# Moving the side work of a hybrid encoder layer to other steps of its weight stream

## The chip, the cores and the metric

The program runs on one core of one Trainium2 chip. The metric is the device time of one execution in microseconds (us), lower is better; of several runs the median counts. The kernel before took 1551.28 us (median of 3 runs, 1549.84 to 1552.31).

## The reference: what is computed

One encoder layer on 256 tokens of width 4096, all in float32.

```python
h = layer_norm(x, emb_g, emb_b)
p = h @ w_in                       # 4096 -> 13312: c_b, c_c, c_h, c_z (2048 each), q (2048), k, v (512 each), a_z (2048)
y_conv = c_b * centred_short_conv(c_c * c_h, conv_w) * silu(c_z)
y_attn = banded_window_attention(q, k, v, sink) * silu(a_z)   # 16 heads of 128, 4 kv heads, window 128, ALiBi
y = concat([y_conv, y_attn]) @ w_out                           # 4096 -> 4096
out = layer_norm(2 ** 0.25 * h + y, ln_g, ln_b)
```

Nearly all arithmetic is in the two projections, `w_in` and `w_out`; their weights are read from memory once. The 256 rows give only two 128-row tiles, so each weight that arrives is used at once and dropped.

## The kernel before, in words

**A stream of weights.** The program is a list of steps (`IN_STEPS`, 304 of them, and 72 `OUT_STEPS`). The output columns are cut into chunks of 512 (26 chunks for `w_in`, in the order K, V, then AZ and Q for each of four groups of heads, then CC, CH, CZ, CB for each of four groups of convolution channels; `w_out` follows). A chunk's contraction of 32 k-tiles is cut into steps of three kinds:

- a *piece* (`s`): four k-tiles, 1 MB of weights, 24 matmuls with 512 columns (`mm`, L241 to L243);
- a *pair* (`S`): two k-tiles multiplied by Strassen's scheme, 0.5 MB, 21 matmuls with 256 columns (`mm_pair`, L265 to L267) where the plain way would need 24 of these;
- a *half* (`h`): two k-tiles the plain way, 12 matmuls with 512 columns.

A chunk of seven pairs runs as `sSShSsSSsSSs` (12 steps). K and V have eight pieces and no pair. A pair needs sums of blocks of the activations, made once for each pair number by `x_sums` (L628), and sums of blocks of the weights, made for each pair by `sums` (L180 to L182).

**Splitting.** Every weight w is split into w_hi and w_lo (`split_hi` on ScalarE, L199; `split_lo` on VectorE, L203), and each product is made of three matmuls: hi with hi, hi with lo, lo with hi. `whi` and `wlo` have three buffers each. So `split_hi(j + 3)` can start when step j's matmuls are done, `split_lo(j + 3)` follows it, and step j + 3 needs both: its first matmul the hi part, its second the lo part.

**What sets the order.** All four engines run their instructions strictly in the order in which the program is written. At step j the loop writes: the matmuls of j (TensorE), `split_hi(j + 3)` (ScalarE), then whatever was entered for step j in a table with `at(step, function)`, then the weight loads (SyncE's queue), then `sums(j + 4)` and `split_lo(j + 3)` (VectorE). The table `later` holds all *side work*: attention, convolution, and the ends of chunks. Work entered at step j therefore stands on TensorE behind the matmuls of j, on ScalarE behind `split_hi(j + 3)`, and on VectorE ahead of `split_lo(j + 3)`.

**The side work.** At a chunk's end `pair_copy` and `pair_sums` (L661, L668 to L671) put the Strassen products together and `whole` (L676, two instructions) adds the plain ones; `whole` belongs to `chunk_end`, written at the first step of the next chunk. Call that step base + 0. From there:

- a CH or CB chunk gets `product` (L681), four transposes on TensorE for each of two halves (L480), and `conv_mul` or `gate_mul` on VectorE;
- a CZ or AZ chunk gets a SiLU on ScalarE (`s_act` L710, `z_act` L523, the latter with a table load), an AZ chunk also transposes (`z_tr`);
- a Q chunk gets a group of four heads, numbered 0 to 3 here. `SPREAD` lists, for each head, the offsets of nine stages: scores (TensorE, L550 to L552), `s_add` (VectorE, L557, L559, L561), `exps` (ScalarE, L570, L571), `recip` (VectorE, L576, L578), `norms` (ScalarE, L584), `p_tr` (four transposes on TensorE, L591, and a copy to `pT` on ScalarE, L593), `p_lo` (VectorE, L598), `pv` (six matmuls, L605 to L607) and `out_z` (VectorE, L611, and a store). The queries are turned and split by `q_tr` and `q_lo` (L540), once for each two heads. A group spreads over two chunks: offsets 0 to 11 lie in the next AZ chunk (or CC), 12 to 23 in the next Q chunk (or CH).

**Buffers that the side work shares.** In the pool `pa` every tile has one buffer, unless it says otherwise: `s` (scores with bias), `pT` (transposed probabilities) and `zT` have one each, `p` has two. PSUM has two buffers named `att`, in turn for the transposed queries, scores, transposed probabilities and `pv`'s result; four `acc` and two `pacc` for the projections.

```python
    ps_att = pps.enter_context(tc.tile_pool(name="ps_att2", bufs=2, space=PSUM))
    pa = ph.enter_context(tc.tile_pool(name="pa", bufs=1))
        t = pa.tile([P, 2, 2, S], F32R, name="pT")
        nc.scalar.activation(t[:, 0, :, :], t_ps, AF.Copy)
```

**The end.** The last two output chunks have 256 columns. `res_load` brings the residual's rows; for the last chunk it issues seven loads on SyncE's queue, ahead of the last weight load.

Of the kernel before, what the change touches and what calls it, by code (L numbers as in the profile page):

```python
# [14 lines left out]
P = 128  # L15
# [25 lines left out]
HW = W // 2  # L41
HT = S // 2
NP = 7
PAIRS = [0, 0] + [NP] * (len(IN_ORDER) - 2)
ORDERS = {0: "s" * 8, NP: "sSShSsSSsSSs"}
OUT = 100
OP = 4
OUT_ORDERS = ["s" * 8] * 2 + ["sSsSsSsSss"] * 4 + ["s" * 8, "", ""]
# [49 lines left out]
def encoder_kernel(ctx: ExitStack, tc: tile.TileContext, x, emb_g, emb_b, wi, ws, conv_w, sink, wo, ln_g, ln_b, out):  # L98
# [516 lines left out]
    def head(n, *steps):  # L615
        return [(t, f, n) for t, f in zip(steps, (scores, s_add, exps, recip, norms, p_tr, p_lo, pv, out_z))]

    SPREAD = [(2, q_tr, 0), (3, q_lo, 0), (7, q_tr, 1), (8, q_lo, 1)] + head(0, 4, 5, 6, 7, 8, 9, 10, 12, 13) + head(
        1, 6, 7, 8, 9, 10, 12, 13, 15, 16) + head(2, 10, 11, 12, 13, 14, 17, 18, 20, 21) + head(
        3, 14, 15, 16, 17, 18, 19, 20, 22, 23)  # L620

    def open_pc():
        nonlocal pc
# [114 lines left out]
    def y_lo(q):  # L738
        for hi, lo, y in y_parts(q):
            nc.vector.tensor_tensor(lo, y, hi.bitcast(F32), op=ALU.subtract)  # L740

    build_tab()
    later = {}

# [6 lines left out]
    def chunk_end(j, ci):  # L751
        c0, fn = next((c, f) for c, f in ENDS if IN_ORDER[ci] >= c)
        g = IN_ORDER[ci] - c0
        fn(ci, g)
        if fn is end_k:
            at(j + 1, k_turn, g)
        if fn is end_cz:
            at(j + 1, s_act)
        if fn is end_z:
            at(j + 1, z_act)  # L760
            for b in range(2):
                at(j + 16 + b, z_tr, b) if g else at(j + 5 + b, z_tr, b)
        if fn is end_q:
            h = g * GROUP
            for t, f, a in SPREAD:
                at(j + t, f, a if f in (q_tr, q_lo) else h + a)
            if g < 2:
                at(j + 15, k_load, g)
                at(j + 23, v_load, g)
        if fn in (end_ch, end_cb):  # L770
            key, other, tr, mul = ("u", "c", conv_tr, conv_mul) if fn is end_ch else ("g", "s", gate_tr, gate_mul)
            last = ci == len(IN_ORDER) - 1
            if last:
                product(key, other)
            else:
                at(j + 2, product, key, other)
            for t, f, b in ((2, tr, 0), (2, tr, 1), (3, mul, 0), (3, mul, 1)) if last else (
                    (4, tr, 0), (5, tr, 1), (5, mul, 0), (7, mul, 1)):
                at(j + t, f, g, b)

    c_ch0 = IN_ORDER.index(C_CH)
# [8 lines left out]
    for j in range(n_pro, N_IN):  # L790
        kind, ci, q = steps[j]
        if j == z0 - 18:
            extra.clear()
        if j == z0 + 6:
            extra.insert(0, (pw, "w6"))
        mm_pair(j) if kind == "pair" else mm(j)
        split_hi(j + 3)
        for fn, a in later.pop(j, []):
            fn(*a)
        if kind == "pair" and q == PAIRS[ci] - 1:  # L800
            pair_copy(ci)
            at(j + 1, pair_sums, ci)
        if ci == 1 and q >= 2 or ci == 2 and j < NPC + 2 + NP:
            x_sums(j - NPC - 2, pa.tile([P, 4 * S], F32, name="xs", tag="zT"))
        if steps[j + 1][1] != ci or j == N_IN - 1:
            if ci == c_ch0:
                at(j + 4, open_pc)
            if PAIRS[ci]:
                at(j + 1, chunk_end, j + 1, ci)
            else:  # L810
                chunk_end(j, ci)
        loads(j)
        sums(j + 4)
        split_lo(j + 3)
# [180 lines left out]
    for n, (c0, w, pk, j0) in enumerate(chunks):  # L995
        us = out_units(n)
        np_ = sum(u[0] == "opair" for u in us)
        for t, (kind, _, q) in enumerate(us):
            j = j0 + t
            if kind == "opair":  # L1000
                mm_pair(j)
            else:
                mm_out(j, n, (0,) if n == ncs - 1 else (0, 1))
            if j + 3 < len(steps):
                split_hi(j + 3)
            for fn, a in later.pop(j, []):
                fn(*a)
            if kind == "opair" and q == np_ - 1:
                pair_copy(OUT + n)
                at(j + 1, pair_sums, OUT + n)  # L1010
                at(j + 1, plus_res, n)
            if j == N_IN + 5:
                open_p2()
            loads(j)
            if j == N_IN + 5:
                res_load(0)
            sums(j + 4)
            if j + 3 < len(steps):
                split_lo(j + 3)
            if t == 0 and n:  # L1020
                for a in ends:
                    end_out2(*a)
                ends = []
                if n < ncs - 1:
                    res_load(n)
            if t == (0 if n == ncs - 1 else 2 if n == ncs - 2 else 4 if n else 7):
                residual(n)
            if n == 2 and t == 4:
                rows_load()
            if n == 2 and t == 8:  # L1030
                rows_split()
                nc.scalar.activation(small.tile([P, 1], F32, name="sd", bufs=1), eps_t, AF.Abs_reciprocal_sqrt)
            if n == ncs - 2 and t == 0:
                res_load(ncs - 1)
        if n < ncs - 1:
            ends = [(n, i, end_out(n, i)) for i in range(2)]
# [81 lines left out]
```

## Time and profile before

| what | value |
|---|---|
| median of 3 runs (lowest to highest) | 1551.28 us (1549.84 to 1552.31) |
| the profiled execution's own time | 1549.91 us |
| its span, from first to last instruction | 1548.2 us |
| TensorE (PE) busy in the span | 1523.4 us (98%) |
| VectorE (DVE) busy | 1327.2 us (86%) |
| ScalarE (ACT) busy | 776.9 us (50%) |
| DMA moved | 315.65 MB, 204 GB/s in the mean |

The profile is of one execution. PE is the matmul row and PEld its weight loads; L199 is line 199 of the kernel. A group's row gives, behind its shape, the count, the busy time and the mean duration of one, and then the time that the engine sat idle just before these instructions, with what ended it. Matmuls overlap: one lasts longer than the distance to the next, so distances are read from start to start. On VectorE and ScalarE an instruction may start up to 0.1 us before the end of the one ahead.

### The profile page before, as it was taken

To read this page: it belongs to the slowest core of one execution; us is meant where nothing else is said; L and a number is where in the kernel's file an instruction comes from. 1 tells how busy PE (TensorE), PEld (TensorE's weight loads), DVE (VectorE), ACT (ScalarE), POOL (GpSimd) and SP (SyncE) were. 2 spreads that over 40 slices of the span, in tenths; PEclk is the share of its full clock that TensorE was granted. 3 is DMA by queue.
4 is the path that set the end of the run, shared out by engine and by line. 5 is a ranking of instruction groups with operands and counts; after the bars stand their busy time and mean duration, and the time that the engine had idled before them with its cause. 6 is when DMAs were issued, how large, how long until landed. Compare 5 with 4: busy or idle time off the path is not lost.

```text
span 1548.2 us, 21816 instructions
## 1 busy us (share of the span) xinstructions
PE 1523.4 (98%) x8870; PEld 1330.6 (86%) x8870; DVE 1327.2 (86%) x1546; ACT 776.9 (50%) x668; POOL 1.3 (0%) x7
## 2 busy tenths in 40 slices
PE   7998999999999999999999999999999999999998
PEld 4887898889888888888888888889888888888897
DVE  8778889898998989988898989898898688888666
ACT  5545556566565554544454455545555444444331
POOL 0000000000000000000000000000000000000000
PEclk9999999999999999999999999999999999999999
DMA  7545555555645456556555555556557756656653
GB/s 293 198 150 204 204 177 186 189 181 193 213 148 206 146 196 238 206 186 224 179 205 203 197 204 197 196 194 225 197 200 271 278 184 225 246 207 233 254 179 141
DMA packets 71716, 315.65 MB, mean 204 GB/s; under 512 B 8544, under 2 KB 12608, under 8 KB 50880
## 3 DMA queue, kind: packets, MB, share of 16 engines
q1 hardware_dynamic: 70608, 312.43, 56.9%
q10 hardware_dynamic: 1008, 1.84, 0.3%
q8 instruction: 69, 1.13, 0.3%
q14 instruction: 31, 0.25, 0.0%
HBM read 305.23 MB, written 8.91 MB: 203 GB/s over the span
## 4 chain that ended last, share of the span: by engine, by line
PE 83%; DVE 8%; ACT 4%; issue 2%; DMA 2%; SPq 0%; ACTq 0%
PE acc L242 13%; PE acc L241 12%; PE acc L243 12%; PE acc L905 7%; PE acc L907 6%; PE acc L906 6%; DVE wlo L203 5%; PE pacc L266 4%; PE pacc L265 4%; PE pacc L267 4%; PE acc L266 3%; PE acc L265 3%; PE acc L267 3%; ACT whi L199 3%; DMA x<-in_x 1%
## 5 line engine op out<-in xcount | busy, mean ns | idle before, releaser
L199 ACT ACTIVATE whi<-w 128x1792 fp32r<-128x1792 f32 (+1 forms) x354 | 620.3, 1753 | 644.2 <-PE acc L243 243.7
L203 DVE TENSOR_TENSOR wlo<-w,whi 128x1792 fp32r<-128x1792 f32 (+1 forms) x354 | 735.6, 2081 | 139.6 <-ACT whi L199 138.9
L242 PE MATMUL acc<-wlo,xT 128*128 128x512 f32 x976 | 384.1, 394 | 6.8 <-DVE wlo L203 6.8
L241 PE MATMUL acc<-whi,xT 128*128 128x512 f32 x976 | 386.2, 396 | 0.0
L243 PE MATMUL acc<-whi,xT 128*128 128x512 f32 x976 | 382.2, 392 | 0.0
L242 PEld LDWEIGHTS acc<-wlo,xT 128*128 128x128 f32 x976 | 183.8, 188 | 46.5 <-DVE wlo L203 10.4
L243 PEld LDWEIGHTS acc<-whi,xT 128*128 128x128 f32 x976 | 183.7, 188 | 41.1
L241 PEld LDWEIGHTS acc<-whi,xT 128*128 128x128 f32 x976 | 183.8, 188 | 36.0
L905 PE MATMUL acc<-whi,xT 128*128 128x512 f32 (+1 forms) x496 | 182.1, 367 | 0.0
L907 PE MATMUL acc<-whi,xT 128*128 128x512 f32 (+1 forms) x496 | 181.7, 366 | 0.0
L906 PE MATMUL acc<-wlo,xT 128*128 128x512 f32 (+1 forms) x496 | 180.5, 364 | 0.0
L180 DVE TENSOR_TENSOR w<-w 128x512 f32<-128x512 f32 x178 | 121.7, 684 | 4.9 <-DMA w<-in_ws 4.9
L907 PEld LDWEIGHTS acc<-whi,xT 128*128 128x128 f32 x496 | 93.1, 188 | 16.3
L906 PEld LDWEIGHTS acc<-wlo,xT 128*128 128x128 f32 x496 | 93.1, 188 | 15.7
L905 PEld LDWEIGHTS acc<-whi,xT 128*128 128x128 f32 x496 | 93.2, 188 | 14.7 <-issue 0.4
L266 PE MATMUL acc<-wlo,xT 128*128 128x256 f32 x368 | 102.7, 279 | 0.0
L265 PE MATMUL acc<-whi,xT 128*128 128x256 f32 x368 | 102.6, 279 | 0.0
L267 PE MATMUL acc<-whi,xT 128*128 128x256 f32 x368 | 102.5, 279 | 0.0
L265 PE MATMUL pacc<-whi,xT 128*128 128x256 f32 x352 | 100.3, 285 | 0.0
L266 PE MATMUL pacc<-wlo,xT 128*128 128x256 f32 x352 | 98.4, 280 | 1.7 <-DVE wlo L203 1.7
L267 PE MATMUL pacc<-whi,xT 128*128 128x256 f32 x352 | 98.1, 279 | 0.0
L266 PE MATMUL pacc<-wlo,SC 128*128 128x256 f32 x336 | 94.7, 282 | 0.0
(236 smaller groups left out, 2040.8 us busy)
## 6 DMA issues: line engine op xcount, KB each, us to landing
w<-in_wi SPq DMA_DIRECT2D x110, 1024.0 KB
w<-in_ws SPq DMA_DIRECT2D x202, 512.0 KB
w<-in_wo SPq DMA_DIRECT2D x43, 1024.0 KB
R<-in_wo SPq DMA_DIRECT2D x13, 1024.0 KB
x<-in_x SPq DMA_DIRECT2D x7, 512.0 KB
yl<-yd SPq DMA_DIRECT2D x7, 512.0 KB
xc<-in_x SPq DMA_DIRECT2D x14, 256.0 KB
R<-in_ws SPq DMA_DIRECT2D x6, 512.0 KB
```

Source lines behind the costliest of these rows:

```text
L180: nc.vector.tensor_tensor(s01, b22, b12.to_broadcast([P, 2, HW]), op=ALU.add)
L199: nc.scalar.activation(part(j, wh[j]), part(j, raw[j]), AF.Copy)
L203: nc.vector.tensor_tensor(part(j, wl[j]), part(j, raw[j]), part(j, wh[j]).bitcast(F32), op=ALU.subtract)
L241: nc.tensor.matmul(a, xh, hk, start=(first and k == 0), stop=False)
L242: nc.tensor.matmul(a, xh, lk, start=False, stop=False)
L243: nc.tensor.matmul(a, xl, hk, start=False, stop=(last and k == PK - 1))
L265: nc.tensor.matmul(o, ah, hi[:, w, :], start=(opens and p == 0), stop=False)
L266: nc.tensor.matmul(o, ah, lo[:, w, :], start=False, stop=False)
L267: nc.tensor.matmul(o, al, hi[:, w, :], start=False, stop=(closes and last))
L905: nc.tensor.matmul(o, yh, hk, start=first, stop=False)
L906: nc.tensor.matmul(o, yh, lk, start=False, stop=False)
L907: nc.tensor.matmul(o, yl, hk, start=False, stop=last)
```

## The change

The diff edits tables of offsets and a few rules. It makes the same products, with one exception in kind: the first chunk with pairs (AZ of group 0) has four pairs and six pieces (`sssSSsSsSs`, 10 steps) in place of seven pairs, a half and four pieces (12 steps), and its `x_sums` are spread over steps 10 to 13 and 17, 20 and 22 in place of steps 10 to 16. `chunk_end` with `whole` goes from base + 0 to base + 3; both SiLUs from base + 1 to base + 4; `product` from base + 2 to base + 4, its transposes from base + 4 and 5 to base + 5 and 6, the multiplications from base + 5 and 7 to base + 7 and 9. All stages of `SPREAD` move, mostly three to five steps later, by different amounts. The loads of k and v for later heads go from base + 15 and 23 to base + 20 and 27. One weight buffer returns a step later (`z0 + 7`), and the residual's loads for the last chunk are written one step later, behind the last weight load.

```diff
--- before.py
+++ after.py
@@ -41,8 +41,9 @@
 HW = W // 2
 HT = S // 2
 NP = 7
-PAIRS = [0, 0] + [NP] * (len(IN_ORDER) - 2)
-ORDERS = {0: "s" * 8, NP: "sSShSsSSsSSs"}
+NP1 = 4
+PAIRS = [0, 0, NP1] + [NP] * (len(IN_ORDER) - 3)
+ORDERS = {0: "s" * 8, NP1: "sssSSsSsSs", NP: "sSShSsSSsSSs"}
 OUT = 100
 OP = 4
 OUT_ORDERS = ["s" * 8] * 2 + ["sSsSsSsSss"] * 4 + ["s" * 8, "", ""]
@@ -615,9 +616,9 @@
     def head(n, *steps):
         return [(t, f, n) for t, f in zip(steps, (scores, s_add, exps, recip, norms, p_tr, p_lo, pv, out_z))]
 
-    SPREAD = [(2, q_tr, 0), (3, q_lo, 0), (7, q_tr, 1), (8, q_lo, 1)] + head(0, 4, 5, 6, 7, 8, 9, 10, 12, 13) + head(
-        1, 6, 7, 8, 9, 10, 12, 13, 15, 16) + head(2, 10, 11, 12, 13, 14, 17, 18, 20, 21) + head(
-        3, 14, 15, 16, 17, 18, 19, 20, 22, 23)
+    SPREAD = [(4, q_tr, 0), (6, q_lo, 0), (10, q_tr, 1), (11, q_lo, 1)] + head(0, 7, 9, 10, 11, 12, 13, 15, 17, 18) + head(
+        1, 9, 10, 11, 13, 14, 16, 18, 19, 21) + head(2, 13, 15, 16, 18, 19, 20, 21, 22, 23) + head(
+        3, 18, 19, 20, 21, 22, 23, 24, 25, 26)
 
     def open_pc():
         nonlocal pc
@@ -739,6 +740,7 @@
         for hi, lo, y in y_parts(q):
             nc.vector.tensor_tensor(lo, y, hi.bitcast(F32), op=ALU.subtract)
 
+    X_SUMS = [NPC + 2 + k for k in range(NP1)] + [2 * NPC + k for k in (1, 4, 6)]
     build_tab()
     later = {}
 
@@ -755,27 +757,27 @@
         if fn is end_k:
             at(j + 1, k_turn, g)
         if fn is end_cz:
-            at(j + 1, s_act)
+            at(j + 4, s_act)
         if fn is end_z:
-            at(j + 1, z_act)
+            at(j + 4, z_act)
             for b in range(2):
-                at(j + 16 + b, z_tr, b) if g else at(j + 5 + b, z_tr, b)
+                at(j + 15 + 2 * b, z_tr, b) if g else at(j + 6 + b, z_tr, b)
         if fn is end_q:
             h = g * GROUP
             for t, f, a in SPREAD:
                 at(j + t, f, a if f in (q_tr, q_lo) else h + a)
             if g < 2:
-                at(j + 15, k_load, g)
-                at(j + 23, v_load, g)
+                at(j + 20, k_load, g)
+                at(j + 27, v_load, g)
         if fn in (end_ch, end_cb):
             key, other, tr, mul = ("u", "c", conv_tr, conv_mul) if fn is end_ch else ("g", "s", gate_tr, gate_mul)
             last = ci == len(IN_ORDER) - 1
             if last:
                 product(key, other)
             else:
-                at(j + 2, product, key, other)
+                at(j + 4, product, key, other)
             for t, f, b in ((2, tr, 0), (2, tr, 1), (3, mul, 0), (3, mul, 1)) if last else (
-                    (4, tr, 0), (5, tr, 1), (5, mul, 0), (7, mul, 1)):
+                    (5, tr, 0), (6, tr, 1), (7, mul, 0), (9, mul, 1)):
                 at(j + t, f, g, b)
 
     c_ch0 = IN_ORDER.index(C_CH)
@@ -791,7 +793,7 @@
         kind, ci, q = steps[j]
         if j == z0 - 18:
             extra.clear()
-        if j == z0 + 6:
+        if j == z0 + 7:
             extra.insert(0, (pw, "w6"))
         mm_pair(j) if kind == "pair" else mm(j)
         split_hi(j + 3)
@@ -800,13 +802,13 @@
         if kind == "pair" and q == PAIRS[ci] - 1:
             pair_copy(ci)
             at(j + 1, pair_sums, ci)
-        if ci == 1 and q >= 2 or ci == 2 and j < NPC + 2 + NP:
-            x_sums(j - NPC - 2, pa.tile([P, 4 * S], F32, name="xs", tag="zT"))
+        if j in X_SUMS:
+            x_sums(X_SUMS.index(j), pa.tile([P, 4 * S], F32, name="xs", tag="zT"))
         if steps[j + 1][1] != ci or j == N_IN - 1:
             if ci == c_ch0:
                 at(j + 4, open_pc)
             if PAIRS[ci]:
-                at(j + 1, chunk_end, j + 1, ci)
+                at(j + (4 if j < N_IN - 1 else 1), chunk_end, j + 1, ci)
             else:
                 chunk_end(j, ci)
         loads(j)
@@ -1030,7 +1032,7 @@
             if n == 2 and t == 8:
                 rows_split()
                 nc.scalar.activation(small.tile([P, 1], F32, name="sd", bufs=1), eps_t, AF.Abs_reciprocal_sqrt)
-            if n == ncs - 2 and t == 0:
+            if n == ncs - 2 and t == 1:
                 res_load(ncs - 1)
         if n < ncs - 1:
             ends = [(n, i, end_out(n, i)) for i in range(2)]
```

The line numbers of the changed kernel are one or two higher than those of the kernel before from L46 on. Three places, as the programs' own order of instructions shows them (names with their buffer numbers; `whi` and `wlo` are the split weights, `w0` to `w8` raw ones).

ScalarE around the `pT` copy of head 1 in the first group, before:

```order
L199 ACTIVATE whi_2115<-w0_2000 128x1024
L593 ACTIVATE pT_2129<-att_2124 128x512
L570 ACTIVATE p_2131,den_2132<-s_2075,nm_2079 128x256 x2
L571 ACTIVATE es_2133<-nm_2079,sk_85 128x2
L199 ACTIVATE whi_2169<-w1_2042 128x1792
L523 ACT_TABLE_LOAD
L523 ACTIVATE z_2040<-z_2040 128x1024
L199 ACTIVATE whi_2203<-w6_2085 128x2048
L584 ACTIVATE p_2131<-p_2131,rd_2175 128x256 x2
```

and in the changed program:

```order
L200 ACTIVATE whi_2179<-w6_2092 128x1792
L594 ACTIVATE pT_2186<-att_2181 128x512
L571 ACTIVATE p_2188,den_2189<-s_2143,nm_2147 128x256 x2
L572 ACTIVATE es_2190<-nm_2147,sk_85 128x2
L524 ACT_TABLE_LOAD
L524 ACTIVATE z_1960<-z_1960 128x1024
L200 ACTIVATE whi_2223<-w2_2121 128x2048
L200 ACTIVATE whi_2260<-w0_2151 128x1792
```

Before, that copy stands at offset 12, and the SiLU at offset 13 behind one more split. Now both stand at offset 16, with the copy first, then the `exps` of head 2, the table load and the SiLU, and only then the split of offset 17, `whi_2223`. The `pv` that last reads `pT` (head 0's) is at offset 12 before, ahead of that copy's transposes on TensorE, and at offset 17 now, behind them.

VectorE around `out_z` of head 0 in the first group (`zT<-att`), before:

```order
L203 TENSOR_TENSOR wlo_2144<-w0_2000,whi_2115 128x1024
L611 TENSOR_TENSOR zT_1441<-att_2117,zT_1441 128x256
L598 TENSOR_TENSOR pT_2129<-att_2124,pT_2129 128x512
L576 TENSOR_TENSOR den_2132<-den_2132,es_2133 128x2
L578 RECIPROCAL rd_2175<-den_2132 128x2
L203 TENSOR_TENSOR wlo_2180<-w1_2042,whi_2169 128x1792
```

and now:

```order
L204 TENSOR_TENSOR wlo_2197<-w6_2092,whi_2179 128x1792
L181 TENSOR_TENSOR w0_2151<-w0_2151 128x512
L182 TENSOR_TENSOR w0_2151<-w0_2151 128x256
L183 TENSOR_TENSOR w0_2151<-w0_2151 128x256
L204 TENSOR_TENSOR wlo_2237<-w2_2121,whi_2223 128x2048
L612 TENSOR_TENSOR zT_1423<-att_2225,zT_1423 128x256
L599 TENSOR_TENSOR pT_2186<-att_2181,pT_2186 128x512
L577 TENSOR_TENSOR den_2189<-den_2189,es_2190 128x2
```

`out_z` stood behind a half's split (1024 wide); it now stands behind the split of `whi_2223`. On TensorE the scores of head 3, which take the `att` buffer that `out_z` of head 0 gives back, are written at offset 18 now, as is `out_z` itself; before they were at 14, and `out_z` at 13.

VectorE after the end of a CB chunk (here the first; `ug` is its tile), before:

```order
L203 TENSOR_TENSOR wlo_6039<-w0_5911,whi_6031 128x1792
L676 TENSOR_TENSOR ug_5998<-acc_5680,ug_5998 128x512
L676 TENSOR_TENSOR ug_5998<-acc_5684,ug_5998 128x512
L180 TENSOR_TENSOR w8_5968<-w8_5968 128x512
L181 TENSOR_TENSOR w8_5968<-w8_5968 128x256
L182 TENSOR_TENSOR w8_5968<-w8_5968 128x256
L203 TENSOR_TENSOR wlo_6076<-w7_5941,whi_6067 128x1024
L203 TENSOR_TENSOR wlo_6105<-w8_5968,whi_6101 128x1792
L681 TENSOR_TENSOR ug_5998<-ug_5998,tm_5637 128x1024
```

and now:

```order
L204 TENSOR_TENSOR wlo_6085<-w2_5952,whi_6078 128x2048
L677 TENSOR_TENSOR ug_5950<-acc_5632,ug_5950 128x512
L677 TENSOR_TENSOR ug_5950<-acc_5636,ug_5950 128x512
L181 TENSOR_TENSOR w1_6021<-w1_6021 128x512
L182 TENSOR_TENSOR w1_6021<-w1_6021 128x256
L183 TENSOR_TENSOR w1_6021<-w1_6021 128x256
L204 TENSOR_TENSOR wlo_6108<-w0_5989,whi_6099 128x1792
L682 TENSOR_TENSOR ug_5950<-ug_5950,tm_5589 128x1024
L204 TENSOR_TENSOR wlo_6136<-w1_6021,whi_6131 128x1792
```

`whole` (the two additions of `acc`) stood four rows ahead of the half's split; it now stands behind the low split for step base + 5 (2048 wide), with `product` one step behind it.

## The prediction

> **What bounds the kernel now.** I read the page first.
>
> ```profile
> span 1548.2 us, 21816 instructions
> PE 1523.4 (98%) x8870; PEld 1330.6 (86%) x8870; DVE 1327.2 (86%) x1546; ACT 776.9 (50%) x668; POOL 1.3 (0%) x7
> ```
>
> TensorE has its matmuls in a row for 98% of the span, so the change can only win back TensorE's waits, and loses where it makes new ones. Those waits stand in the view of waits and in the group of the `p_tr` transposes:
>
> ```profile
> PE acc L242 <- DVE wlo L203: 6.8, 11, 2.8
> PE pacc L266 <- DVE wlo L203: 1.7, 1, 1.7
> PE acc L906 <- DVE w L203: 1.4, 1, 1.4
> ACT pT L593 <- PE att L607: 14.1, 4, 3.5
> ```
>
> ```profile
> L591 PE MATMUL att<-ident,p 128*128 128x128 f32 x64 | 11.8, 286 | 1.2 <-ACT p L584 0.5
> ```
>
> The first three are late low splits; the fourth is a wait of ScalarE that costs TensorE nothing today, and it decides this forecast. Then I read the timeline at a group's third and fourth head, TensorE first, then ScalarE (start, duration, engine, line):
>
> ```profile
> 274.59 0.60 PE L591 MATMUL att<-ident,p 128*128 128x128 f32 x4
> 274.95 0.36 PE L265 MATMUL pacc<-whi,xT 128*128 128x256 f32 x1
> ...
> 280.31 0.94 PE L591 MATMUL att<-ident,p 128*128 128x128 f32 x4 [0.17 <-ACT p L584]
> 281.01 0.48 PE L241 MATMUL acc<-whi,xT 128*128 128x512 f32 x1
> ...
> 286.60 0.28 PE L605 MATMUL att<-pT,v 128*128 128x256 f32 x1
> 287.31 0.28 PE L265 MATMUL pacc<-whi,xT 128*128 128x256 f32 x1
> ...
> 292.25 0.28 PE L605 MATMUL att<-pT,v 128*128 128x256 f32 x1
> ```
>
> ```profile
> 282.32 1.71 ACT L199 ACTIVATE whi<-w 128x1792 fp32r<-128x1792 f32 x1 [1.66 <-issue]
> 287.56 0.60 ACT L593 ACTIVATE pT<-att 128x512 fp32r<-128x512 f32 x1 [3.54 <-PE att L607]
> ```
>
> Head 3's transposes end before 281.01, yet the copy to `pT` starts at 287.56: `pT` has one buffer, and head 2's `pv` (286.60 to 287.31) still reads it. Only splits stand behind the copy on ScalarE, the next for a step that is two pairs and a `pv` away, so nothing comes late. The rows also give unit times: a pair 2.47 (two from 287.31 to 292.25), a piece 5.5 (281.01 to 286.60, less a 0.1 restart), six `pv` or scores matmuls 0.71, four transposes 0.36.
>
> **What the change removes.** The idle in the rows above is 6.8 + 1.7 + 1.4 + 1.2 = 11.1. A row's idle counts from the modelled end of a matmul, 0.16 later than the next start would be, and the restart takes 0.1 more: 13 late splits times 0.27 is 3.5. The waiting `p_tr` takes 0.70 from 280.31 to 281.01 where the undisturbed one takes 0.36; with the wait ahead about 0.5 a time, eight times 4.2, of which 1.2 is counted. The longest waits also cost clock. The stretches after the V chunk (columns: window, its length, busy times, granted clock, DMA):
>
> ```profile
> 124.70:127.90 3.20, 0.39 (x4) 0.06 (x2) 3.06 (x6) 1.03 (x1) 0.00 (x0) 0.93 0.64 264
> 127.90:130.60 2.70, 2.70 (x6) 2.13 (x7) 2.00 (x2) 2.47 (x2) 0.00 (x0) 0.50 0.57 193
> ```
>
> After 2.8 us without matmuls the clock is 0.50 for 2.7 us: 1.35 lost. Together 11.1 + 3.5 + 3.0 + 1.35 = 18.9. All of it can go: seven `x_sums` no longer stand in consecutive steps beside the end of V, `norms` get a piece or two steps before `p_tr`, `product` leaves the split of base + 5, the SiLUs leave base + 1, and the last weight load leaves the queue behind seven small loads (1.4). Bounds 14 (`p_tr` and its restarts kept) and 19.
>
> **What it adds.** *Matmuls.* The first AZ chunk goes from 4 pieces, 7 pairs and a half (22.0 + 17.3 + 2.75) to 6 pieces and 4 pairs (33.0 + 9.9): 0.9.
>
> *The `pT` wait with a queue behind it.* `p_tr` of head 1 is now written at offset 16, `pv` of head 0 at 17, behind a piece. So ScalarE's copy waits for that `pv`, and behind it in ScalarE's queue stand the `exps` of head 2, the table load, the SiLU and the split of offset 17. VectorE's split waits for that one, `out_z` of head 0 stands behind it, and the scores of head 3 on TensorE wait for `out_z`'s `att` buffer, one pair after the `pv`. The durations, ScalarE then VectorE:
>
> ```profile
> 258.24 0.50 ACT L570 ACTIVATE p<-s,nm 128x256 f32<-128x256 f32 x1
> ...
> 259.23 0.28 ACT L571 ACTIVATE es<-nm,sk 128x2 f32<-128x2 f32 x1
> ...
> 261.93 1.28 ACT L523 ACT_TABLE_LOAD   x1
> 263.23 1.06 ACT L523 ACTIVATE z<-z 128x1024 f32<-128x1024 f32 x1
> 264.19 1.90 ACT L199 ACTIVATE whi<-w 128x2048 fp32r<-128x2048 f32 x1
> ```
>
> ```profile
> 266.12 2.29 DVE L203 TENSOR_TENSOR wlo<-w,whi 128x2048 fp32r<-128x2048 f32 x1 [0.63 <-ACT whi L199]
> 268.33 0.68 DVE L557 SCALAR_TENSOR_TENSOR s<-tab,att 128x512 f32<-128x512 f32 x1
> ...
> 269.91 0.69 DVE L180 TENSOR_TENSOR w<-w 128x512 f32<-128x512 f32 x1
> ...
> 292.21 0.42 DVE L611 TENSOR_TENSOR zT<-att,zT 128x256 f32<-128x256 f32 x1
> ```
>
> From the pair's start: copy at 0.25 (as 287.56 against 287.31), 0.50 to the next instruction (its 0.60 less the usual overlap of 0.1), `exps` 0.99 (258.24 to 259.23) and 0.25, load 1.30, SiLU 0.96, split 1.90, low split 2.24, `out_z` 0.42: 8.8. TensorE arrives at 2.47 and waits 6.3. The last group has no SiLU there (its next chunk is CC): 8.8 - 2.26 - 2.47 = 4.1. Sum 3 x 6.3 + 4.1 = 23.0. From below the nearest row is head 3's wait today, which costs 0; from above 29, if the queue behind it starts 1.5 later each time. I take 23.0, since every duration has a row.
>
> *VectorE falls behind in offsets 9 to 15.* Take zero at the start of step 9's matmuls. The split for step 11 ends at about 4.4 (0.25 + 1.90 + 2.24). Then come `s_add` 1.58 (268.33 to 269.91), `sums` 1.52, a split 2.21: 9.7. `s_add` of head 1 needs the only `s` tile back from the `exps` of head 0 in the same step, which stand on ScalarE behind a split that needs those `sums` (7.5 + 1.71), a copy 0.5, the table load 1.3 and 0.95: 12.0, so VectorE idles 2.3. Then 1.58 + 1.52 + 1.94 (step 10), 0.6 + 0.3 + 1.77 + 1.94 (step 11, `q_lo` and `pair_sums` of 0.42 each), 1.52 + 1.14, 0.3 + 1.94, 1.52 + 2.21, and `p_lo` of head 0 0.69: 31.0. TensorE comes to `p_tr` of head 1, which needs the `att` buffer that `p_lo` gives back, after two pieces, five pairs, a half, two scores and two sets of transposes: 11.0 + 12.35 + 2.75 + 1.42 + 0.72 = 28.2. It waits 2.8, there or at step 13, whose pair needs `pacc` from `pair_sums`; in later groups some of it overlaps other extra work of TensorE. I take 2.6 x 4 = 10.4, between 0 (as at these stages today) and 14.
>
> *Ends of chunks.* The first CB end (DVE rows, then PE):
>
> ```profile
> 679.06 2.03 DVE L203 TENSOR_TENSOR wlo<-w,whi 128x1792 fp32r<-128x1792 f32 x1 [1.07 <-ACT whi L199]
> 681.00 1.22 DVE L681 TENSOR_TENSOR ug<-ug,tm 128x1024 f32<-128x1024 f32 x1
> 682.13 0.69 DVE L180 TENSOR_TENSOR w<-w 128x512 f32<-128x512 f32 x1
> ...
> 683.65 2.29 DVE L203 TENSOR_TENSOR wlo<-w,whi 128x2048 fp32r<-128x2048 f32 x1
> ```
>
> ```profile
> 684.77 0.60 PE L480 MATMUL att<-ident,ug 128*128 128x128 f32 x4
> ```
>
> In the changed order 681.00 is followed by `sums` 1.52, split 2.21, `whole` 1.20 (two instructions on tiles as large as that of 682.13, 0.69 with 0.09 overlapped), `sums` 1.52, split 1.94 and `product` 1.22: 690.6. TensorE reaches its transposes after base + 5, at 684.77 + 5.5 = 690.3. So the low split is in time, and the transposes wait about 0.4 in its place: six ends, 2.4 (0 to 4.6, today's 0.77 each). `q_tr` one step behind `whole` waits the same way: `whole` ends at 686.0, TensorE comes at 684.8, so 1.2 in the first group, about 0.6 in the three where `pv` and `z_tr` come between: 3.0 (0 to 4.8).
>
> *Clock.* Four waits of 4 to 6 us, longer than the 2.8 us that cost 1.35: 5.4. [...]
>
> **The sum.** Added 0.9 + 23.0 + 10.4 + 2.4 + 3.0 + 5.4 = 45.1, removed 18.9: 26.2 more than the profiled execution's 1549.91 us, 1576. The median of the runs is 1.4 above that execution: 1577.
>
> **The rivals.** *Absorbed.* The `pT` wait costs TensorE nothing, as today: if the low split behind it came within one pair's 2.47 us, the scores would not wait, and there would be no cold clock. For it: today's four waits of 3.5. Against it: it decides from a queue of 2.2 us between copy and split on, and this queue is 8.8. Then 16.7 is added and 18.9 removed: 1549, no slower than before. *The plan works*: every stage is hidden and VectorE keeps up, since at 86% it has room over the whole span: 1551.3 - 18.9 + 0.9 = 1533. Against it: its 2.3 us idle at `s_add` and the backlog of 2.8 have rows. *Long half clock.* After each wait of TensorE the clock stays at 0.50 until the second of two nearby waits is over, 6 to 8 us instead of 2.7: 4 x 3.5 more, 1591. For it: the 2.8 wait at `p_tr` lies one piece ahead of the 6.3. Against it: after 127.9 one spell of 2.7 was enough. *Half of it*: the long wait lets VectorE catch up, so that the 10.4 and 3.0 go: 1564.
>
> **Chances.** The forecast 70%, half of it 9%, long half clock 11%, absorbed 5%, the plan 5%. Range 1560 to 1591: it holds the first three. 0.2% (3 us) is about what a measurement of this kernel can tell from no change. Slower 0.91 (the first three and a little of absorbed), same 0.04, faster 0.05.
>
> **What would show it.** Right: the scores' first matmul (L551) has about 20 us of idle ahead of it, four waits of 4 to 6.5, put down to `out_z` (L612); the granted clock dips four times between 270 and 600 us; `p_tr` (L592) or a pair waits for VectorE before them; the low splits' 6.8 and 1.4 are nearly gone; from the first CC chunk on only 0.4 is seen at `ug`'s transposes. Wrong: the scores start within 0.2 us of the pair's end, or the four groups of heads together take less than 20 us more.

## The result, and the profile after

The changed kernel takes 1585.41 us (median of 4 runs, 1584.81 to 1586.58) against 1550.72 (4 runs, 1549.84 to 1552.31) beside it: a ratio of 1.0223, 95% interval 1.0206 to 1.0241. It is slower, by 35 us where 26 were forecast. TensorE's old stalls are gone and new, longer ones have come. First the page, then the view of waits of the changed kernel (its line numbers are one or two higher):

```profile
span 1583.6 us, 21740 instructions
PE 1535.5 (97%) x8843; PEld 1339.4 (85%) x8843; DVE 1320.1 (83%) x1535; ACT 774.8 (49%) x666; POOL 1.3 (0%) x7
```

```profile
PE att L551 <- DVE zT L612: 22.7, 4, 6.3
ACT pT L594 <- PE att L608: 5.3, 4, 2.6
PE att L592 <- DVE pT L599: 6.8, 4, 2.3
DVE s L558 <- ACT p L571: 6.1, 4, 2.6
PE pacc L266 <- DVE z L669: 1.5, 1, 1.5
PE acc L243 <- DVE wlo L204: 0.2, 1, 0.2
```

TensorE's waits for late low splits (6.8 before) are down to 0.2. The scores of head 3 wait four times for `out_z`, `p_tr` of head 1 four times for `p_lo`. The timeline at the first of the scores' waits, ScalarE, then VectorE, then TensorE:

```profile
268.94 1.71 ACT L200 ACTIVATE whi<-w 128x1792 fp32r<-128x1792 f32 x1 [5.38 <-DVE w L183]
271.57 0.60 ACT L594 ACTIVATE pT<-att 128x512 fp32r<-128x512 f32 x1 [0.93 <-PE att L608]
272.06 0.50 ACT L571 ACTIVATE p<-s,nm 128x256 f32<-128x256 f32 x1
...
273.34 1.28 ACT L524 ACT_TABLE_LOAD   x1
274.63 1.06 ACT L524 ACTIVATE z<-z 128x1024 f32<-128x1024 f32 x1
275.60 3.48 ACT L200 ACTIVATE whi<-w 128x2048 fp32r<-128x2048 f32 x2
```

```profile
263.80 0.68 DVE L599 TENSOR_TENSOR pT<-att,pT 128x512 fp32r<-128x512 f32 x1
264.40 0.68 DVE L558 SCALAR_TENSOR_TENSOR s<-tab,att 128x512 f32<-128x512 f32 x1
...
265.97 1.28 DVE L677 TENSOR_TENSOR z<-acc,z 128x512 f32<-128x512 f32 x2
...
268.34 0.42 DVE L183 TENSOR_TENSOR w<-w 128x256 f32<-128x256 f32 x1
...
277.52 2.29 DVE L204 TENSOR_TENSOR wlo<-w,whi 128x2048 fp32r<-128x2048 f32 x1 [3.30 <-ACT whi L200]
279.73 0.42 DVE L612 TENSOR_TENSOR zT<-att,zT 128x256 f32<-128x256 f32 x1
```

```profile
280.20 0.58 PE L551 MATMUL att<-kT,qhl 128*128 128x256 f32 x1 [6.26 <-DVE zT L612]
```

The chain is the predicted one, link by link: copy 271.57, `exps` 272.06, table load 273.34, SiLU 274.63, split 275.60, low split 277.52, `out_z` 279.73, scores 280.20. But the bracket behind the copy says that ScalarE stood idle only 0.93 us for `pv`; until 270.64 it was in a split that had itself waited for VectorE's `sums` (268.34, behind `p_lo`, `s_add` and the `whole` of z). So two theories stood after the result. **Hold** (the prediction's): the copy, held by `pv`, starts the chain. **Queue**: the chain would start nearly as late without the hold, because VectorE is behind already and the exponentials, the load and the SiLU lie between two splits.

The clock took more than forecast. The clock records change in steps of 3.41 us. The stretches around that wait, cut in these steps (window, its length, busy times of TensorE, its weight loads, VectorE, ScalarE, GpSimd, then the granted clock and the DMA's share and rate):

```profile
272.35:275.77 3.42, 1.59 (x14) 1.39 (x12) 1.80 (x4) 3.40 (x8) 0.00 (x0) 1.00 0.81 290
275.77:279.18 3.41, 0.00 (x0) 0.00 (x0) 1.66 (x1) 3.31 (x2) 0.00 (x0) 1.00 0.29 120
279.18:282.59 3.41, 2.39 (x11) 2.39 (x12) 3.31 (x9) 0.00 (x0) 0.00 (x0) 0.50 0.38 77
282.59:286.01 3.42, 3.42 (x18) 3.42 (x18) 3.35 (x4) 0.00 (x0) 0.00 (x0) 0.50 0.78 295
```

The half clock holds for two steps, 6.83 us. Between the start-up and the last matmul, the clock records of this execution show five spells at 0.50: from 279.18, 381.58, 487.39 and 593.20, at the scores' waits, 6.83 us each, and from 579.55, after `p_tr`'s longest wait, 3.41 us. Matmuls that started in them came 11.0 us later than at full clock (start to start, against 0.229 us for 512 columns, 0.117 for 256 and 0.109 for a transpose).

### The profile page after: what moved, and what is told of

It reads as the page before. It is cut to its first block, busy times and chain, and to the rows that moved or that the text cites. A ratio compares the mean times of both kernels' runs of the same rounds, so it can differ in the third digit from the quotient of the medians.

```text
span 1583.6 us, 21740 instructions
## 1 busy us (share of the span) xinstructions
PE 1535.5 (97%) x8843; PEld 1339.4 (85%) x8843; DVE 1320.1 (83%) x1535; ACT 774.8 (49%) x666; POOL 1.3 (0%) x7
## 4 chain that ended last, share of the span: by engine, by line
PE 57%; DVE 5%; ACT 1%; DMA 1%; issue 0%; SPq 0%; ACTq 0%
PE acc L242 7%; PE acc L243 7%; PE acc L244 7%; PE acc L907 6%; PE acc L909 6%; PE acc L908 6%; PE pacc L267 3%; PE pacc L266 3%; PE pacc L268 3%; DVE wlo L204 3%; PE acc L266 2%; PE acc L267 2%; PE acc L268 2%; ACT whi L200 1%; DMA w<-in_ws 1%; DVE w L181 1%
## 5 line engine op out<-in xcount | busy, mean ns | idle before, releaser
L200 ACT ACTIVATE whi<-w 128x2048 fp32r<-128x2048 f32 (+1 forms) x352 | 617.6, 1756 | 694.5 <-DVE w L183 221.2
L204 DVE TENSOR_TENSOR wlo<-w,whi 128x2048 fp32r<-128x2048 f32 (+1 forms) x352 | 733.1, 2085 | 181.5 <-ACT whi L200 179.8
L242 PE MATMUL acc<-whi,xT 128*128 128x512 f32 x988 | 392.1, 397 | 0.0
L243 PE MATMUL acc<-wlo,xT 128*128 128x512 f32 x988 | 388.4, 393 | 0.2 <-DVE wlo L204 0.2
L244 PE MATMUL acc<-whi,xT 128*128 128x512 f32 x988 | 388.5, 393 | 0.0
```

Of the source, the lines that this page charges most:

```text
L200: nc.scalar.activation(part(j, wh[j]), part(j, raw[j]), AF.Copy)
L204: nc.vector.tensor_tensor(part(j, wl[j]), part(j, raw[j]), part(j, wh[j]).bitcast(F32), op=ALU.subtract)
L242: nc.tensor.matmul(a, xh, hk, start=(first and k == 0), stop=False)
L243: nc.tensor.matmul(a, xh, lk, start=False, stop=False)
L244: nc.tensor.matmul(a, xl, hk, start=False, stop=(last and k == PK - 1))
```

## The experiments

**1. Two buffers for `pT`.** The hold can't occur.

```diff
-        late = pa.tile([P, 2, 2, S], F32R, name="klate", tag="pT")
+        late = pa.tile([P, 2, 2, S], F32R, name="klate", tag="pT", bufs=2)
...
-        t = pa.tile([P, 2, 2, S], F32R, name="pT")
+        t = pa.tile([P, 2, 2, S], F32R, name="pT", bufs=2)
```

> One edit on the changed kernel: two buffers for pT. Two theories of the scores' waits (L551, 6.42, 6.42, 6.42 and 4.07 us). Hold (the prediction's): ScalarE's copy for head 1 is held by head 0's pv, and all that stands behind it starts that late. Then the copy now starts right after its transposes, a piece earlier, the four waits (23.3) and the half clock after them (27 us at 0.50, 13.6 lost) go: 1585.4 - 36.9 = 1548. Queue (rival): the copy would start late anyway, since the split ahead of it on ScalarE ends only 0.93 us before it in the first group (the row of the pT wait: 5.3 in four); exps, table load, SiLU and the next split and low split alone make the wait. Then at most 5.3 goes, the four waits stay at 5 us or more, the half clock too: 1580 to 1585.

Measured: 1581.62 us, ratio 1.0202 (1.0187 to 1.0218). ScalarE's timeline at the same place, and the wait:

```profile
268.65 1.71 ACT L200 ACTIVATE whi<-w 128x1792 fp32r<-128x1792 f32 x1 [5.39 <-DVE w L183]
270.25 0.58 ACT L594 ACTIVATE pT<-att 128x512 fp32r<-128x512 f32 x1
```

```profile
PE att L551 <- DVE zT L612: 20.8, 4, 5.2
```

The copy now follows the split at once, and the scores' wait only falls from 6.42 to 5.38 in the first three groups. There the queue theory stands, and the hold was worth about 1 us a group. The last group decides nothing: the hold had been 2.6, yet the wait grew from 4.07 to 5.35, because the next weights came 2.2 us late for `sums` (1.35 in the changed kernel), and TensorE arrived sooner, since this time no half clock followed `p_tr`'s wait (1.00 in the step from 574.74, where the changed kernel has 0.50 in the step from 579.55).

**2. `out_z` of head 0 one step earlier**, so that it stands ahead of the late low split.

```diff
-    SPREAD = [(4, q_tr, 0), (6, q_lo, 0), (10, q_tr, 1), (11, q_lo, 1)] + head(0, 7, 9, 10, 11, 12, 13, 15, 17, 18) + head(
+    SPREAD = [(4, q_tr, 0), (6, q_lo, 0), (10, q_tr, 1), (11, q_lo, 1)] + head(0, 7, 9, 10, 11, 12, 13, 15, 17, 17) + head(
```

> One edit on the changed kernel: out_z of head 0 one step earlier (18 to 17), so it stands ahead of the late low split on VectorE. Both theories: the scores of head 3 wait no more. If only they depended on that low split, 36.9 goes: 1548. If the late low split itself is the cause, the next one behind it is p_lo of head 1, and pv of head 1 on TensorE waits for it, a set of scores and a pair (3.2 us) later: a wait of about 3.5 us in three groups and 1.5 to 2 in the last, 12.5 in all in place of 23.3. Clock: where a wait of 3.5 us makes a spell of 3.4 us at 0.50 (as waits of 2.5 and 2.8 us did), the four spells lose 5.1 in place of 13.6: 1585.4 - 10.8 - 8.5 = 1566; where it makes one of 6.8 us, 1571.

Measured: 1571.6 us, ratio 1.0137 (1.0122 to 1.0153).

```profile
PE att L606 <- DVE den L577: 11.4, 4, 3.4
```

The scores wait no more, but six matmuls and a pair later `pv` of head 1 waits for `p_lo`, which stood behind the same low split (the row names `recip`, the instruction after `p_lo`): 3.60 three times, 1.25 in the last group. Here the stall of 6.42 behind the late low split came back as 3.60 at the next instruction behind it, with 3.2 us of work in between.

**3. The SiLU one step later**, behind the split of offset 17.

```diff
-            at(j + 4, z_act)
+            at(j + 5, z_act)
```

> One edit on the changed kernel: z_act (the table load and the SiLU) one step later, behind the split of offset 17. If ScalarE's queue is the path, the scores' waits in the first three groups shrink by the load and the SiLU, 2.3 each, to about 4.1, and the last stays at 4.1: 6.9 less. A wait of 4.07 was followed by 6.8 us at 0.50, so the clock's loss stays: 1578.5. If the SiLU is not on the path (the wait is set by VectorE's own backlog): 1585.

Measured: 1580.0 us, ratio 1.0195 (1.0180 to 1.0210).

```profile
PE att L551 <- DVE zT L612: 15.6, 4, 3.9
```

The first three waits fell from 6.42 to 4.07, by 2.35: the 1.28 of the table load and the 1.06 of the SiLU, to 0.01. So ScalarE's queue is the path. Part of the gain was given back in the first group, where the transposes of z (`z_tr`) waited 2.0 for the SiLU.

**4. Two buffers for `s`.**

```diff
-        ti = pa.tile([P, 2, S], F32, name="ti", tag="s")
+        ti = pa.tile([P, 2, S], F32, name="ti", tag="s", bufs=2)
...
-        s = pa.tile([P, 2, S], F32, name="s")
+        s = pa.tile([P, 2, S], F32, name="s", bufs=2)
```

> One edit on the changed kernel: two buffers for s. If VectorE's wait for the only s tile (6.1 us in four groups) is what makes p_lo and pair_sums late, the waits of p_tr (7.46) and of the pairs at pacc (2.3) shrink by about 6 together, the scores' waits stay at 6.4 (the queue behind them starts from the same place): 1579. If VectorE is behind by its sheer work: 1585. If the scores' wait is a backlog that the earlier one feeds, it shrinks too, and the clock's loss with it: below 1575.

Measured: 1576.96 us, ratio 1.0177 (1.0157 to 1.0198).

```profile
PE att L592 <- DVE pT L599: 3.0, 4, 1.3
PE att L551 <- DVE zT L612: 24.0, 4, 6.3
```

`s_add` no longer waits, `p_tr`'s waits fall from 6.8 to 3.0, the one at `pacc` is gone, and the scores' waits do not shrink (6.42 three times; the last grew from 4.07 to 5.42): TensorE comes to them earlier too.

**5. Work for TensorE in the wait.** What the scores wait for stays as it is; only the idle time is filled.

```diff
-        o_ps = st_["o", h] = ps_att.tile([P, S], F32, name="att")
+        full = ps_att.tile([P, 2, S], F32, name="att")
+        o_ps = st_["o", h] = full[:, 0, :]
+        st_["full", h] = full
...
+    def warm(h):
+        for _ in range(48 if h < 12 else 30):
+            nc.tensor.transpose(st_["full", h][:, 1, 0:P], ident, ident)
+
-    SPREAD = [(4, q_tr, 0), (6, q_lo, 0), (10, q_tr, 1), (11, q_lo, 1)] + head(0, 7, 9, 10, 11, 12, 13, 15, 17, 18) + head(
+    SPREAD = [(18, warm, 0), (4, q_tr, 0), (6, q_lo, 0), (10, q_tr, 1), (11, q_lo, 1)] + head(0, 7, 9, 10, 11, 12, 13, 15, 17, 18) + head(
```

> The changed kernel with 48 extra 128x128 transposes (30 in the last group; 0.109 us each, 5.2 and 3.3 us) on TensorE ahead of the scores of head 3, into an unused half of pv's PSUM tile: TensorE works in the wait and what it waits for is untouched. If the half clock comes from TensorE's idleness, the four spells after these waits (27 us at 0.50, 13.6 lost) go, and the scores start when they did: 1585.4 - 13.6 = 1572, with only the 3.4 us spell after p_tr's wait of 2.5 left. If the clock falls for another reason (what the other engines do, the place in the program), the spells stay and the time is 1585.

Measured: 1578.13 us, ratio 1.0188 (1.0172 to 1.0203). A stretch with the fillers and the one behind it:

```profile
276.00:279.50 3.50, 2.58 (x24) 2.35 (x22) 2.57 (x3) 2.49 (x2) 0.00 (x0) 1.00 0.12 52
279.50:286.00 6.50, 6.39 (x44) 5.97 (x45) 6.33 (x12) 2.50 (x3) 0.00 (x0) 1.00 0.72 232
```

The clock stays at 1.00, where the changed kernel had 0.50 from 279.18 to 286.01, and its mean over the span is 0.998 against 0.990, which makes some 6 us at half clock in place of 31 (an estimate from these means and the spans). So the half clock at the scores' waits came from TensorE's idleness. The gain was 7.3 by the medians, smaller than the 13.6 that I had expected, for two reasons. The spells begin while TensorE still waits, so of their 27 us only some 20 had matmuls in them: they cost 9.6, and the stretch from 200 to 600 us is indeed 9.1 shorter. And in the profiled execution, the slowest of the four (1580.59), some 3.1 was lost again behind 600 us and 1.9 after the last matmul. Of the 3.1, a wait of 1.26 at a late low split shows 0.9 (0.34 in the changed kernel); ahead of it a weight load had come 4.0 late for `sums`. The rest is open.

**6. The change without its attention part**: the table of heads and the ends of the Q chunks as before, all else as in the change.

```diff
-    SPREAD = [(4, q_tr, 0), (6, q_lo, 0), (10, q_tr, 1), (11, q_lo, 1)] + head(0, 7, 9, 10, 11, 12, 13, 15, 17, 18) + head(
...
+    SPREAD = [(2, q_tr, 0), (3, q_lo, 0), (7, q_tr, 1), (8, q_lo, 1)] + head(0, 4, 5, 6, 7, 8, 9, 10, 12, 13) + head(
...
-                at(j + (4 if j < N_IN - 1 else 1), chunk_end, j + 1, ci)
+                at(j + (4 if j < N_IN - 1 and not C_Q <= IN_ORDER[ci] < C_K else 1), chunk_end, j + 1, ci)
```

> All of the change but the attention: the stages of the heads and the ends of the Q chunks stand as in the kernel before, the first AZ chunk has four pairs, SiLUs, convolution, chunk ends, x_sums and the residual stand as in the changed kernel. By the ledger: before 1549.9, less 6.8 + 2.9 of late low splits and their restarts, less 1.7 of clock (one spell of 3.4 us), less 1.4 at the end, plus 0.9 of matmuls and 2.2 at the ends of chunks: 1540; the waits of the heads' p_tr stay (about 4). If the rest loses too (VectorE behind at the ends of chunks): 1550 or more.

Measured: 1550.86 us, ratio 1.0008 (0.9998 to 1.0018), no difference, where 1540 was expected if the rest only won. ScalarE's timeline ahead of a `p_tr` that began at 275.20, then the group of `p_tr`:

```profile
269.82 1.06 ACT L524 ACTIVATE z<-z 128x1024 f32<-128x1024 f32 x1
...
274.65 0.89 ACT L585 ACTIVATE p<-p,rd 128x256 f32<-128x256 f32 x2
```

```profile
L592 PE MATMUL att<-ident,p 128*128 128x128 f32 x64 | 11.8, 286 | 6.4 <-ACT p L585 5.9
```

Between 100 and 200 us, in V and the first AZ chunk, it wins 7.4 us of TensorE's waiting. From 200 to 600 us it loses 7.3, most of it at `p_tr` of head 3, which waits for `norms`; in the first three groups the SiLU with its table load now stands ahead of these on ScalarE.

**7. The kernel before with the changed table alone.** `k_load` and `v_load` stay at offsets 15 and 23, ahead of head 3's scores and `pv` (18, 25), so head 3 of the first two groups works on later keys and values; its instructions are the same.

```diff
-    SPREAD = [(2, q_tr, 0), (3, q_lo, 0), (7, q_tr, 1), (8, q_lo, 1)] + head(0, 4, 5, 6, 7, 8, 9, 10, 12, 13) + head(
...
+    SPREAD = [(4, q_tr, 0), (6, q_lo, 0), (10, q_tr, 1), (11, q_lo, 1)] + head(0, 7, 9, 10, 11, 12, 13, 15, 17, 18) + head(
...
```

> The kernel before with the table of the attention's stages alone; chunk ends, SiLUs, convolution, first AZ chunk, x_sums and the residual as before. If the table carries the loss by itself: the waits of the scores without the SiLU in ScalarE's queue (it stands at offset 13 here) 4.1 to 5.4 four times, 16 to 22; VectorE's backlog at p_tr and at pacc 8 to 17; four to six spells of half clock of 3.4 or 6.8 us, 7 to 17; less 4 of p_tr's old waits: 1549.5 + 27 to 52, 1577 to 1600. If the loss needs the later chunk ends and SiLU as well: 1565 or less.

Measured: 1598.26 us, ratio 1.0318 (1.0303 to 1.0334).

```profile
PE att L550 <- DVE zT L611: 19.9, 4, 5.3
PE att L591 <- DVE pT L598: 11.4, 4, 3.0
```

The table carries the loss by itself; the rest of the change takes more than a quarter of it back. And here, by the trace, the hold does decide. The SiLU stands at offset 13, ScalarE is early, and it waits for `pv`:

```profile
ACT pT L593 <- PE att L607: 14.2, 4, 4.9
```

In the first group it stands idle for 3.45, and behind the copy come a table load (now that of the exponentials), `exps`, split and low split: 5.49 for the scores. By the trace the hold and VectorE's backlog are two ways into the same queue; in the full change, with its later SiLU and chunk ends, the backlog is nearly as late. No run took the hold away from the table alone, so this is read and not tried.

**8. The rest without the AZ chunks' part too**: `chunk_end`, `z_act` and `z_tr` of AZ as before.

```diff
-                at(j + (4 if j < N_IN - 1 else 1), chunk_end, j + 1, ci)
+                at(j + (1 if IN_ORDER[ci] >= C_Q or j == N_IN - 1 else 4), chunk_end, j + 1, ci)
...
-            at(j + 4, z_act)
+            at(j + 1, z_act)
...
-                at(j + 15 + 2 * b, z_tr, b) if g else at(j + 6 + b, z_tr, b)
+                at(j + 16 + b, z_tr, b) if g else at(j + 5 + b, z_tr, b)
```

> rest_only with the ends of the AZ chunks, their SiLU and z_tr where the kernel before has them too. rest_only came out at 1550.9 (1.0008 of before): it won 7.3 in the first AZ chunk and lost as much at p_tr of head 3 in every group (1.75 against 0.36 us ahead of it, and 3.4 us at half clock once). If the SiLU at offset 16, ahead of the norms of head 3 on ScalarE, makes those waits, they go here: 1550.9 - 4 x 1.4 - 1.5 = 1544. If the four-pair first chunk or the later convolution ends make them, 1551.

Measured: 1546.24 us, ratio 0.9976 (0.9967 to 0.9986): 4.6 us below experiment 6.

```profile
L592 PE MATMUL att<-ident,p 128*128 128x128 f32 x64 | 11.8, 286 | 2.6 <-ACT p L585 2.0
```

The waits of `p_tr` for `norms` fell from 5.9 to 2.0 in all, and the mean granted clock is 1.000 (0.999 in experiment 6). So the later end of the AZ chunks had made most of them. Which part of it is not shown, because the run moves two things back together: the SiLU, which stood ahead of `norms` on ScalarE, and `whole` of z (1.28), which stood on VectorE ahead of the `sums` that ScalarE's split waits for. In the last group a CC chunk follows, without a SiLU but with its `whole` still at the later step, and there the wait stays: 1.30 in experiment 6 and 1.40 here, against 0.31 before, start to start. So the SiLU is not all of it.

**9 and 10. Another table of heads.** If order is all that is wrong, an order without these collisions must be fast. Two were made, from the changed kernel:

```diff
-    SPREAD = [(4, q_tr, 0), (6, q_lo, 0), (10, q_tr, 1), (11, q_lo, 1)] + head(0, 7, 9, 10, 11, 12, 13, 15, 17, 18) + head(
...
+    SPREAD = [(5, q_tr, 0), (6, q_lo, 0), (10, q_tr, 1), (10, q_lo, 1)] + head(0, 8, 8, 9, 11, 11, 12, 13, 15, 17) + head(
+        1, 7, 9, 11, 13, 14, 16, 17, 19, 22) + head(2, 13, 13, 13, 16, 18, 21, 22, 23, 24) + head(
+        3, 18, 19, 19, 20, 20, 23, 24, 25, 25)
...
-                    (5, tr, 0), (6, tr, 1), (7, mul, 0), (9, mul, 1)):
+                    (6, tr, 0), (7, tr, 1), (8, mul, 0), (9, mul, 1)):
...
-                at(j + (4 if j < N_IN - 1 else 1), chunk_end, j + 1, ci)
+                at(j + (5 if C_Q <= IN_ORDER[ci] < C_K else 4 if j < N_IN - 1 else 1), chunk_end, j + 1, ci)
```

That is 9; it also has the two buffers for `s` of experiment 4. Experiment 10 has one, the same convolution offsets, the Q ends at 1 in place of 5, and this table:

```diff
+    SPREAD = [(3, q_tr, 0), (4, q_lo, 0), (8, q_tr, 1), (9, q_lo, 1)] + head(0, 6, 6, 6, 7, 7, 9, 10, 11, 11) + head(
+        1, 5, 7, 9, 10, 10, 12, 13, 15, 16) + head(2, 10, 10, 12, 13, 13, 15, 17, 19, 20) + head(
+        3, 13, 14, 14, 17, 17, 19, 19, 22, 23)
```

> The changed kernel with another table of the heads (each out_z and p_lo ahead of the low splits that were late, stages that wait for each other further apart), two buffers for s, the Q ends one step later and the convolution's transposes one step behind product. If all that the changed kernel loses are the waits of its ledger (scores 23.3, p_tr 7.5, pacc 2.3, q_tr 2.3, ug 2.2) and the clock's 11.0 after them, none of which is needed by the amount of work: 1585.4 - 48.5 = 1537. If VectorE's work between offsets 9 and 20 is too much wherever it stands, waits move to other stages: 1549 or more.

> As table_b, but with one buffer for s, and the Q ends where the kernel before has them (one step behind the chunk), so that the heads start three offsets earlier and end earlier. If the waits come from the order alone and not from the single s tile: 1537 to 1539, as table_b. If the s tile's single buffer must cost something, p_tr's and pacc's waits stay (7.5 + 2.3) with a spell of half clock: 1548.

Measured: 1533.54 us, ratio 0.9899 (0.9886 to 0.9913), and 1535.52 us, ratio 0.9908 (0.9895 to 0.9922). Both beat the kernel before and the changed one. The page of the first, and its groups of `p_tr` and of the scores:

```profile
span 1531.4 us, 21737 instructions
PE 1517.7 (99%) x8843; PEld 1328.9 (87%) x8843; DVE 1319.0 (86%) x1535; ACT 775.7 (51%) x666; POOL 1.3 (0%) x7
...
PE 98%; DVE 1%; DMA 0%; ACT 0%; SPq 0%; issue 0%; ACTq 0%
```

```profile
L592 PE MATMUL att<-ident,p 128*128 128x128 f32 x64 | 9.6, 272 | 0.0
L551 PE MATMUL att<-kT,qhl 128*128 128x256 f32 x32 | 9.0, 281 | 0.0
```

VectorE is as busy as in the changed kernel (1319.0 against 1320.1), and TensorE has no idle ahead of these two groups; the mean granted clock is 1.000, against 0.990. The work fitted all along. In experiment 10 VectorE waits nowhere for the single `s` tile, so no second buffer is needed where the stages that share it stand apart; the 2 us between the two tables were not traced.

## Why the prediction was right, and where not

It forecast slower, 1577, with 1585.4 inside its range. Taken by its steps (sizes from start to start of matmuls in the changed kernel's profiled execution):

| step | predicted | measured |
|---|---|---|
| matmuls added | 0.9 | 0.9 (36 more of 512 columns, 63 fewer of 256, at 0.229 and 0.117) |
| scores of head 3 | 6.3, 6.3, 6.3, 4.1 = 23.0 | 6.42, 6.42, 6.42, 4.07 = 23.3 |
| VectorE behind (`p_tr`, `pacc`) | 10.4 | 7.5 + 2.3 = 9.8 |
| `q_tr` | 3.0 | 2.2 |
| ends of chunks (`ug`) | 2.4 | 2.1, and 0.7 at two late low splits not forecast |
| clock | 5.4 | 11.0 |
| removed | 18.9 | 18.4 |
| not in the sum | 0 | 3.8 |

One term was mis-sized, and it makes most of the 8 us that are missing. **The clock's 5.4**: the step "four waits of 4 to 6 us, longer than the 2.8 us that cost 1.35" took one spell of before as the price of every spell. That spell was one step, 3.41 us (127.43 to 130.84 in the clock records). The spells at the scores' waits were twice as long (2.7, 1.6, 2.4 and 2.9 lost), and a fifth came after a wait of 2.5 (1.4). The mean over the five is 2.2.

**"All of it can go"** was right: the kernel before loses 9.2 at late low splits in the input chunks, 1.9 at a pair behind V, 1.6 at the last weight, 4.2 at `p_tr` of its heads and 1.5 by its half clock, 18.4 together. In the changed kernel all of these delays are gone but 0.4 at the first CB end, which is in the 0.7 above. **What the sum lacks**: the span grew by 35.4, while the added terms make 50.0 and the removed 18.4, which leaves 3.8. Of this, 0.8 is the first matmul's later start, and about 2.4 comes from some 3800 matmuls with 512 columns that stood 0.6 ns further apart in this execution: at full clock 229.5 ns in the mean from start to start, against 229.0 before. What sets this distance is open.

**The reason behind the 23.0** held in its chain and its durations and failed in its first link. The prediction let the copy to `pT` start the queue because `pv` holds it. Experiment 1 took the hold away and 5.38 of 6.42 stayed: the split ahead of the copy was late as well, from VectorE's backlog. The two came to within a microsecond of each other in the first three groups, so it is partly luck that this number came out right; in the table alone (experiment 7) the trace shows the hold as the later one. For the last group the 4.1 was met (4.07), but experiment 1 shows that another wait, for weights, lies just behind the hold. That the chain is ScalarE's queue was right (experiment 3).

**VectorE falls behind** through the `s` tile: right (experiment 4 takes away 6.1 of the 9.8). That the changed Q ends and stages would not be hidden at `ug` and `q_tr` was right in sign, and the sizes came within 0.8.

**The rivals.** "Absorbed" and "the plan works" fell. "Half of it" fell: `p_tr`'s and the scores' waits stood together in all groups. "Long half clock" had the right length, 6.8 us, and the wrong condition: in the first group the clock was at 1.00 until 279.18, late in the second wait, and then at 0.50 for 5.80 us of work behind that wait. Each such spell cost 1.6 to 2.9, not 4.9.

**The steps of the clock.** The spells at the first three of the scores' waits start at 279.18, 381.58 and 487.39, that is 102.40 and 105.81 us apart: 30 and 31 steps of 3.413 us.

## What to carry to other kernels

When work of several engines is moved to other steps, follow each queue past the step, since a stage is as late as the latest instruction ahead of it, and a wait that is taken away can come back at the next instruction behind the same late one (experiment 2: 3.60 in place of 6.42). A long stall of a TensorE-bound kernel can cost more than itself: here five stalls of 2.5 to 6.4 us were each followed by half clock and lost 11.0 us more. Price such a stall by whole spells as the trace shows them, here 3.41 or 6.83 us at 0.50. And before giving up on an order as too full, compare the engine's busy time: here nearly the same VectorE work cost 50 us more in one order than in another.

## What the runs showed that was not expected

How long the clock stayed at half went with where the wait fell in the 3.41 us steps, more than with its length. A wait of 5.38 ended 0.05 us after a step began, and cost one step (two `pT` buffers):

```profile
480.66:485.99 5.33, 0.15 (x2) 0.00 (x0) 3.07 (x4) 4.24 (x3) 0.00 (x0) 1.00 0.53 192
485.99:489.40 3.41, 3.37 (x16) 3.37 (x16) 3.31 (x7) 0.00 (x0) 0.00 (x0) 0.50 0.67 178
489.40:491.00 1.60, 1.60 (x15) 1.60 (x15) 1.57 (x3) 0.00 (x0) 0.00 (x0) 1.00 0.83 348
```

A wait of 4.07 that reached 0.69 into a step cost two (the changed kernel, its last group), and one of 3.15 that reached 0.56 into a step cost one (the table alone, experiment 7):

```profile
593.20:596.61 3.41, 2.72 (x12) 2.72 (x13) 3.31 (x9) 0.00 (x0) 0.00 (x0) 0.50 0.49 147
596.61:600.03 3.42, 3.42 (x17) 3.42 (x17) 3.05 (x4) 0.00 (x0) 0.00 (x0) 0.50 0.69 256
```

```profile
271.56:274.97 3.41, 2.86 (x9) 2.50 (x10) 3.27 (x7) 0.00 (x0) 0.00 (x0) 0.50 0.47 159
274.97:277.00 2.03, 2.03 (x10) 1.65 (x10) 2.03 (x3) 1.71 (x1) 0.00 (x0) 1.00 0.00 0
```

So a step at half clock with 2.86 of 3.41 us of matmuls was followed by full clock, one with 2.72 by a second step at half. The other cases lie on the two sides of these: 2.88 (experiment 3, from 588.51), 2.95 (the kernel before, from 127.43), 3.37 (two `pT` buffers) and 3.41 (the changed kernel, from 579.55) were followed by full clock; 0.00, 1.77 and 2.39 (the changed kernel, from 381.58, 487.39 and 279.18) were not. What starts a spell is less sharp. In the kernels before and after, between the start-up and the last matmul, each step at full clock with 1.07 us of matmuls or less was followed by half clock and none with 1.59 or more was (the step from 272.35 above has 1.59). In the run with two `pT` buffers a step with 1.56 (from 571.32) was not followed by half clock either, but in experiment 6 one with 1.75 (from 272.92) was. By these cases the same kernel can lose a few microseconds more or less by where its waits happen to fall (an estimate from the 1.4 to 2.9 that a spell cost in the changed kernel).
